# One encoder block on one core: gates moved ahead of the weight splits, GpSimd's tile work taken out of the token tiles and the tail, the router in one fp32 product

## The chip, the core and the metric

The kernel runs on one core of a Trainium2 chip. The metric is the device time of one execution in microseconds; before the change the median of three runs is 2175.32 us (2174.38 to 2176.11). The engines are named as the profile names them: PE is TensorE (PEld is its weight load), DVE is VectorE, ACT is ScalarE, POOL is GpSimd and SP is SyncE, which here only issues DMAs.

## The reference, cut to what matters

The block takes x (1024 tokens x 1024 channels) and computes, in fp32:

- h = RMSNorm(x), z = h @ w_in, whose columns are q, k, v and the two halves a and b of a convolution group.
- Attention over 8 heads with three dilated windows (this part is not touched).
- conv = swish(LayerNorm(depthwise_conv(a * sigmoid(b)))), with a width of 31 over 512 channels.
- x1 = x + concat(attn, conv) @ w_out.
- h2 = RMSNorm(x1) with weight norm2_g; aff = softmax(h2 @ w_router) over 16 experts; each expert takes its 128 highest tokens; y = (silu(h2 @ w1) * (h2 @ w3)) @ w2 for them, times the affinity, added into x1 at the tokens' rows.

## The kernel before

Matrix products of fp32 data are made from two fp32r halves. A tile is split into hi (an ACT copy that rounds) and lo (the difference from the raw tile, on DVE or POOL), and a product is three matmuls: hi*hi, hi*lo, lo*hi (`mm3`, lines 113 to 115). The order of the instructions on PE, ACT and DVE is the program's order (`manual_schedule`); each engine takes its queue in order. POOL's and SP's instructions are placed by the scheduler of the framework, and wait for their tiles.

The stages on which the change bears:

- **Projection and convolution (to about 181 us).** The conv channels are done in four blocks of 128, i = 0 to 3. For each block `z_ab` (line 409) makes b (part 0) and a (part 1), 48 matmuls of 512 columns each. `glu` (line 293) is a generator: b times the norm factor on DVE and a sigmoid on ACT, twice; then the gate times the factor and the product with a on DVE, twice; then a split of the result and 16 DMAs that spread it into the tile U. `conv` (line 329) has nine steps of 12 matmuls. After each step it splits the weights of four steps later (`wc_split`: ACT hi, DVE lo, then a load into the freed ring place from POOL's queue), and after the fifth, ACT copies the first half of the sums out (`left`, line 336). The generator of block i runs one step after each step of conv(i - 1), so that sigmoids and weight splits alternate in ACT's queue. The splits of the next w_ab block (`split_ab`) stand ahead of the loop. The last conv, conv(3), comes after the copy-out and squares of the first q tile.
- **Output projection, token tiles t = 0 to 7 (456.9 to about 593 us).** For each tile of 128 tokens PE makes 48 matmuls of 512 columns (`product`, line 1067), DVE adds the residual (line 1072), and the previous tile gets its norm (`norm`), its transposes (`turned`: 4 PE transposes, an ACT hi copy, an ACT raw copy, a POOL subtraction, line 1092, twice), its router (16 fp32r matmuls whose stationary side is the 32 columns of the split weights, an ACT copy, a PE transpose back, two DVE additions), its softmax, and `kept`: h2 = x1 * r on ACT, times norm2_g on POOL (line 1104), then a DMA to the DRAM tile h2s. In between, DVE sorts the affinities of earlier tiles (`ranked`, with `MAX8`, `MATCH_REPLACE8` and the max/min pairs of lines 986 and 988), in portions that `drip` puts between the other instructions by fixed counts (`DW`, `DL`).
- **The tail (593 to 638.7 us).** The last tile's norm, router and softmax, the last sort, the selection of the 128 tokens of each expert, and the gather of the first expert's rows by an indirect DMA from POOL (line 1412). In this stretch the first two weight tiles of the experts are split with POOL's subtraction (`split_next`), the third on DVE after the indices are known (line 1400).
- **Experts (638.7 us to the end).** For each of 16 experts the gathered rows are transposed (`transposed`: 8 PE transposes, two ACT hi copies and two DVE subtractions of 512 columns), and 33 weight tiles of 128x2048 are loaded, split (lines 1195 and 1196) and multiplied. `load_to` loads them into a ring; a load waits until the tile that had its place is split.

Of the kernel before, what the change touches and what calls it, by code (L numbers as in the profile page):

```python
# [68 lines left out]
def build(ctx, tc, nc, I, out):  # L69
# [77 lines left out]
    wr = sm([P, 8, 2, NE], F32R, "wr")  # L147
# [21 lines left out]
    def router_weights():  # L169
        V.tensor_tensor(wrr, wrr, g2t[:, :, None].to_broadcast([P, 8, NE]), op=ALU.mult)  # L170
        split(wrr, wr[:, :, 0], wr[:, :, 1])
# [121 lines left out]
    def glu(i, pab):  # L293

        sg = sm([P, 2, 512], F32, "sg", tag="tmp4", bufs=1)
# [3 lines left out]
        for half in range(2):  # L299
            c = slice(512 * half, 512 * half + 512)  # L300
            V.tensor_tensor(sg[:, half], pab[0][:, half], rbc[:, c], op=ALU.mult)
            A.activation(sg[:, half], sg[:, half], AF.Sigmoid)
            yield
        ufp = uf.rearrange("p (r t) -> p t r", r=4)
        for half in range(2):
            c = slice(512 * half, 512 * half + 512)
            V.tensor_tensor(sg[:, half], sg[:, half], rbc[:, c], op=ALU.mult)
            V.tensor_tensor(ufp[:, 128 * half:128 * half + 128],
                            pab[1][:, half].rearrange("p (t r) -> p t r", r=4),
                            sg[:, half].rearrange("p (t r) -> p t r", r=4), op=ALU.mult)  # L310
            yield
# [120 lines left out]
    for i in range(4):  # L432
        pab = pab_next
        if i == 0:
            z_ab(0, pab, ((0, 0), (1, 0), (0, 1), (1, 1)))
            pab_next = [psC("pb")]
            A.activation(zeros[:, 0, 1:2], g1[:, 0:1], AF.Sigmoid)
            z_ab(1, pab_next, ((0, 0), (0, 1)), norms_out)
        else:
            if i == 1:  # L440
                pab.append(psS("pa"))
                z_ab(1, pab, ((1, 0), (1, 1)))

                for _ in split_ab(2):
                    pass
                pab_next = [psS("pb")]
                z_ab(2, pab_next, ((0, 0), (0, 1)))
            elif i == 2:
                pab.append(psS("pa"))
                z_ab(2, pab, ((1, 0), (1, 1)))  # L450
            else:
                pab = [psS("pb"), psS("pa")]
                z_ab(i, pab, ((0, 0), (0, 1), (1, 0), (1, 1)))
        while ends:
            ends.pop(0)()
        if i == 2:
            for _ in split_ab(3):
                pass
# [7 lines left out]
        if i == 0:  # L466
            for _ in gates:
                pass
            for n in range(4):
                wc_split(n)  # L470
            continue
        if i == 3:
# [76 lines left out]
    for c in range(2):  # L549
        raw = load_pieces(c + 1)  # L550
        for tp in range(4):
            ps = psS("pqk")
            z_pair(ps, tp, w)
            while ends:
                ends.pop(0)()
# [28 lines left out]
            if (c, tp) == (0, 0):  # L584
                for _ in conv(3, ends):
                    pass
# [377 lines left out]
    misc = slot(4, [D + 2 * P + NT + 2 * NE + 5 * P], F32, "misc")  # L964
    g2 = misc[:, 0:D]
    nc.sync.dma_start(g2, I["g2"].partition_broadcast(P))
    cs = misc[:, D:D + 2 * P + NT + 2 * NE]
# [4 lines left out]
    W, gt, eq = (misc[:, D + 2 * P + NT + 2 * NE + i * P:][:, 0:P] for i in range(3))  # L972
    run = misc[:, D + 5 * P + NT + 2 * NE:].rearrange("p (a k) -> p a k", a=2)
# [55 lines left out]

    xf = misc[:, D + 2 * P + NT + 2 * NE:][:, 0:512]  # L1030
    h2T = slot(11, [2, 8, P], F32R, "h2T")
    ORDER = (0, 1, 4, 5, 2, 6, 7, 3)

    class Token:


        def __init__(self, t):
            self.t, self.xt, self.h2, self.h2T = t, xt2[:, t % 2], h22[:, t % 2], h2T
# [41 lines left out]
        def turned(self, j0, j1, between=None):  # L1080
# [3 lines left out]
            hh, hl = (self.h2T[:, i, j0:j1].rearrange("p j t -> p (j t)") for i in range(2))  # L1084
            A.activation(hh, pt[:, 0:n], AF.Copy)
            if between:
                between()
            if self.last and j0 >= 4:
                V.tensor_tensor(hl, pt[:, 0:n], hh.bitcast(F32), op=ALU.subtract)
            else:  # L1090
                A.activation(xf[:, 0:n], pt[:, 0:n], AF.Copy)
                G.tensor_tensor(hl, xf[:, 0:n], hh.bitcast(F32), op=ALU.subtract)
# [9 lines left out]
        def scaled(self):  # L1102
            A.activation(self.h2[:, 0:D], self.xt, AF.Copy, scale=self.r)
            G.tensor_tensor(self.h2[:, 0:D], self.h2[:, 0:D], g2, op=ALU.mult)

        def router(self, j0=0, j1=8):

            if j0 == 0:
                self.pr = psM("pr")
            for part in range(2):  # L1110
                for j in range(j0, j1):
                    w_ = wr[:, j].rearrange("p a e -> p (a e)")
                    T.matmul(self.pr[0:2 * NE, 0:P], w_, self.h2T[:, part, j], start=j == 0 and not part,
                             stop=j == 7 and part == 1)
            if j1 == 8:
                self.lT = pack[0:2 * NE, (3 + self.t % 2) * P:(4 + self.t % 2) * P]
                A.activation(self.lT, self.pr[0:2 * NE, 0:P], AF.Copy)

        def logits(self):
            pl = psM("pl")  # L1120
            T.transpose(pl[:, 0:2 * NE], self.lT, ident[0:2 * NE, 0:2 * NE])
            self.lg = lg = sm([P, NE], F32, "lg", tag="lg", bufs=2)
            self.sc = sm([P, 4], F32, "rsc", tag="rsc", bufs=2)
            V.tensor_copy(lg, pl[:, 0:NE])
            yield
            V.tensor_tensor(lg, pl[:, NE:2 * NE], lg, op=ALU.add)
            yield
            V.tensor_reduce(self.sc[:, 0:1], lg, axis=AX.X, op=ALU.max)

        def softmax(self, between=lambda: None, prev=None):  # L1130
# [3 lines left out]
            A.activation(af, self.lg, AF.Exp, scale=self.r, bias=sc[:, 1:2], accum_out=sc[:, 2:3])  # L1134
# [178 lines left out]
    prev.kept()  # L1313
# [4 lines left out]
    def split_next(n=1):  # L1318
        for _ in range(n):
            if ahead:  # L1320
                ahead.pop(0)()
# [6 lines left out]
    split_next()  # L1328
    cur.router(6, 8)
    split_next()  # L1330
# [9 lines left out]
    cur.spread()  # L1340
    cur.kept()
    split_next(npre * 2)
# [17 lines left out]
    T.transpose(pt[:, 0:P], half, ident)  # L1360
    drain()
# [24 lines left out]
    for t in range(NT):  # L1386
        T.matmul(rows[:, t * P:(t + 1) * P], to_b[:, t], pos, start=True, stop=True)

# [11 lines left out]
    split_part(npre, 0, 2048, V)  # L1400
# [15 lines left out]
    def transposed(e, xe):  # L1416
        xT = slot(XT[e % 2], [2, 8, P], F32R, "xTe")
        for q in range(2):
            pt = psT("xeT")
            for j in range(4):  # L1420
                T.transpose(pt[:, j * P:(j + 1) * P], xe[:, (4 * q + j) * P:(4 * q + j + 1) * P], ident)  # L1421
            hh = xT[:, 0, 4 * q:4 * q + 4].rearrange("p j t -> p (j t)")
# [104 lines left out]
def layouts(inputs):  # L1527
# [7 lines left out]
    L["g2"] = c(f["norm2_g"].reshape(1, D))  # L1535
# [66 lines left out]
```

## Time and profile before

| what | value |
|---|---|
| median of the timed runs | 2175.32 us |
| the profiled execution, its own time | 2172.52 us |
| its span from first to last instruction | 2170.7 us |
| mean granted PE clock | 0.982 of full |
| busy: PE, DVE, ACT, POOL | 2083.0, 1755.5, 1397.7, 231.0 us |
| chain that ended last | PE 87%, DVE 6%, issue 3%, DMA 2% |

The page gives busy time by engine, a timeline in 40 slices and the chain of work that ended last. Shares over the whole span mix the experts' stage, which is more than two thirds of it, with the stages before it, so the rows below are taken stage by stage. In a timeline row the first number is the start, the second the duration; a group of several instructions is one row with its count, and the bracket at the end says how long the engine was idle before and what released it. A busy matmul is not a matmul at its peak: ends are modelled and overlap the next start, so the pitch from start to start is the cost of one.

### The profile page before, as it was taken

The numbers are of one execution on the slowest core, as the hardware profiler recorded it, in microseconds if no ns is written. First come the engines' busy times: TensorE is split into PE (matmuls) and PEld (weight loads), VectorE is DVE, ScalarE is ACT, GpSimd is POOL, SyncE is SP. The second block draws the span as 40 slices with busy tenths as digits, with TensorE's granted clock in tenths as the row PEclk, the third lists the DMA queues.
The fourth block names the chain that finished last, engine by engine and source line by source line (L and its number), as shares of the span: only waits on it lengthen the run. The fifth ranks groups of instructions, "written<-read, shape, count | busy, mean of one in ns | idle before, by whom it ended". The sixth has DMA issues, their size and how long they took to land.

```text
span 2170.7 us, 27853 instructions
## 1 busy us (share of the span) xinstructions
PE 2083.0 (96%) x10458; PEld 1748.3 (81%) x10458; DVE 1755.5 (81%) x2231; ACT 1397.7 (64%) x1465; POOL 231.0 (11%) x169
## 2 busy tenths in 40 slices
PE   9899999988849999999999999999999999999997
PEld 7888889976638888888888888888888888888886
DVE  6435847868968888888888888888888888888886
ACT  5334735553337777777777777777777777777774
POOL 2110001233230101010010001011010101101010
PEclk9999999999959999999999999999999999999998
DMA  8540158844459999999999999999999999999990
GB/s 290 141 132 25 40 145 168 161 131 178 183 212 346 357 392 371 382 379 374 380 361 387 375 379 384 370 382 363 386 374 376 388 371 382 359 388 378 376 358 10
DMA packets 138743, 647.71 MB, mean 298 GB/s; under 512 B 47984, under 2 KB 52464, under 8 KB 68592
## 3 DMA queue, kind: packets, MB, share of 16 engines
q1 hardware_dynamic: 130688, 617.48, 76.7%
q0 software_dynamic: 7776, 28.45, 4.7%
q8 instruction: 82, 1.34, 0.3%
q14 instruction: 53, 0.43, 0.1%
q10 hardware_dynamic: 144, 0.00, 0.0%
HBM read 607.69 MB, written 21.40 MB: 290 GB/s over the span
## 4 chain that ended last, share of the span: by engine, by line
PE 87%; DVE 6%; issue 3%; DMA 2%; ACT 1%; POOL 0%; SPq 0%; POOLq 0%; ACTq 0%; DVEq 0%
PE w L113 15%; PE w L115 15%; PE w L114 15%; PE y L115 7%; PE y L113 7%; PE y L114 7%; PE pqk L503 4%; PE po L834 2%; PE pv L503 2%; PE hT L1445 2%; PE wo L1067 1%; PE pp L814 1%; PE sc L775 1%; PE sc L776 1%; DVE top L988 1%
## 5 line engine op out<-in xcount | busy, mean ns | idle before, releaser
L1196 DVE TENSOR_TENSOR w<-rw,w 128x2048 fp32r<-128x2048 f32 x527 | 1196.0, 2285 | 183.3 <-ACT w L1195 178.9
L1195 ACT ACTIVATE w<-rw 128x2048 fp32r<-128x2048 f32 (+1 forms) x531 | 1006.9, 1910 | 274.9 <-PE w L115 138.9
L113 PE MATMUL w<-w,xTe 128*128 128x512 f32 (+1 forms) x1536 | 584.4, 380 | 0.0
L115 PE MATMUL w<-w,xTe 128*128 128x512 f32 (+1 forms) x1536 | 574.8, 374 | 0.0
L114 PE MATMUL w<-w,xTe 128*128 128x512 f32 (+1 forms) x1536 | 574.5, 374 | 0.0
L115 PEld LDWEIGHTS w<-w,xTe 128*128 128x128 f32 x1536 | 289.3, 188 | 54.6 <-DVE xTe L1424 0.2
L114 PEld LDWEIGHTS w<-w,xTe 128*128 128x128 f32 x1536 | 289.8, 189 | 51.4
L113 PEld LDWEIGHTS w<-w,xTe 128*128 128x128 f32 x1536 | 289.5, 188 | 51.1 <-ACT xTe L1423 0.4
L115 PE MATMUL y<-w,hts 128*128 128x512 f32 x700 | 276.7, 395 | 0.0
L113 PE MATMUL y<-w,hts 128*128 128x512 f32 x700 | 275.5, 394 | 0.0
L114 PE MATMUL y<-w,hts 128*128 128x512 f32 x700 | 275.2, 393 | 0.0
L114 PEld LDWEIGHTS y<-w,hts 128*128 128x128 f32 x700 | 131.9, 188 | 30.6
L115 PEld LDWEIGHTS y<-w,hts 128*128 128x128 f32 x700 | 131.9, 188 | 29.3
L113 PEld LDWEIGHTS y<-w,hts 128*128 128x128 f32 x700 | 131.9, 188 | 29.1
L1447 ACT ACTIVATE hts<-hT 128x512 fp32r<-128x512 f32 x95 | 53.7, 565 | 112.5 <-PE hT L1445 112.5
L1481 POOL DMA_INDIRECT out_dram<-xy,idx x16 | 78.8, 4927 | 422.9 <-DVE xy L1480 343.5
L1412 POOL DMA_INDIRECT xy<-h2s,idx x16 | 17.6, 1101 | 892.1 <-PE xeT L1421 678.8
L503 PE MATMUL pqk<-wqkv,hT 128*128 128x512 f32 x384 | 89.6, 394 | 0.0
L503 PEld LDWEIGHTS pqk<-wqkv,hT 128*128 128x128 f32 x384 | 72.1, 188 | 16.5
L834 PEld LDWEIGHTS po<-VAB,pT 128*128 128x128 f32 x496 | 59.5, 193 | 5.6 <-DVE pT L818 2.7
L834 PE MATMUL po<-VAB,pT 128*128 128x65 f32 x496 | 59.9, 273 | 4.2 <-DVE pT L818 2.1
L1506 DVE TENSOR_TENSOR sg<-w,sg 128x512 f32<-128x512 f32 x96 | 61.4, 640 | 0.0
(271 smaller groups left out, 2293.0 us busy)
## 6 DMA issues: line engine op xcount, KB each, us to landing
rw<-in_w SPq DMA_DIRECT2D x525, 1024.0 KB
wcraw<-in_wconv POOLq DMA_DIRECT2D x36, 256.0 KB, 4.0
KK<-stg SPq DMA_DIRECT2D x16, 512.0 KB
rawqkv<-in_w_qkv SPq DMA_DIRECT2D x6, 1024.0 KB
h2s<-h SPq DMA_DIRECT2D x8, 520.0 KB
xr<-in_xT SPq DMA_DIRECT2D x8, 512.0 KB
xs<-in_x SPq DMA_DIRECT2D x4, 1024.0 KB
U<-st SPq DMA_DIRECT2D x64, 64.0 KB
```

What stands on the lines that cost most here:

```text
L113: T.matmul(ps, xh, wh, start=start, stop=False)
L114: T.matmul(ps, xh, wl, start=False, stop=False)
L115: T.matmul(ps, xl, wh, start=False, stop=stop_)
L503: T.matmul(ps[:, k], hT[j][:, a % 2, tok], w[j // 2][:, a // 2, j % 2], start=j == 0 and a == 0, stop=j == 7 and a == 2)
L775: T.matmul(ps[:, i, c], q, kh, start=True, stop=False)
L834: T.matmul(po[:, i * VW:(i + 1) * VW], pt[:, i, c], v, start=c == 0, stop=c == 1)
L1195: A.activation(wh, raws[i][:, c0:c1], AF.Copy)
L1196: E.tensor_tensor(wl, raws[i][:, c0:c1], wh.bitcast(F32), op=ALU.subtract)
L1445: T.transpose(pt[:, k * P:(k + 1) * P], h[:, k * P:(k + 1) * P], ident)
L1447: A.activation(hh, pt[:, 0:w], AF.Copy)
L1481: G.indirect_dma_start(out=out[:, :], out_offset=bass.IndirectOffsetOnAxis(ap=idx[:, e:e + 1], axis=0), in_=ys, in_offset=None, compute_op ...
L1506: V.tensor_tensor(sg[:, 0:w], pb[:, 0:w], sg[:, 0:w], op=ALU.mult)
```

## The change

1. `glu` is cut in two. `glu_gate` (b times the factor, sigmoid, times the factor, for both halves) stands right after b is made, ahead of `split_ab`; `glu` keeps the product with a, the split and the spread, one step after each of the first four conv steps. The PE order becomes: a of block i (with the last transposes of conv(i - 2) between its two halves), b of block i + 1, conv(i - 1). Two steps of conv(3) are put ahead of the first q tile's copy-out.
2. The POOL subtraction and the POOL multiplication by norm2_g in the token tiles go. h2s now holds x1 * r without norm2_g; norm2_g is multiplied at the experts' transposes, one 128-column piece at a time. The broadcast load of norm2_g (512 KB) goes.
3. The router is one fp32 product with the tokens as stationary side (8 matmuls of 16 columns into a 128 x 16 tile); the copy, the transpose back and the two additions go, and softmax reads PSUM.
4. The first weight tile's split goes to two halves on DVE, one after the transposes of the last sort, one after the rows' matmuls; the second tile's goes to DVE after the indices, ahead of the third. `kept` of tile 6 moves behind the last tile's `spread`.

```diff
-    for i in range(4):
-        pab = pab_next
...
-        gates = glu(i, pab)
...
+    A.activation(zeros[:, 0, 1:2], g1[:, 0:1], AF.Sigmoid)
+    z_ab(0, pab_next, ((0, 0), (1, 0), (0, 1), (1, 1)))
+    pab, pab_next = pab_next, [psC("pb")]
+    z_ab(1, pab_next, ((0, 0), (0, 1)), norms_out)
+    glu_gate(0, pab[0])
+    for _ in glu(0, pab[1]):
+        pass
+    for n in range(4):
+        wc_split(n)
+    for i in range(1, 4):
+        pab = pab_next
+        glu_gate(i, pab[0])
+        if i == 3:
...
+        else:
+            for _ in split_ab(i + 1):
                 pass
+        pab.append(psS("pa"))
+        z_ab(i, pab, ((1, 0),))
+        end()
+        z_ab(i, pab, ((1, 1),))
+        gates = glu(i, pab[1])
+        if i < 3:
+            pab_next = [psS("pb")]
+            z_ab(i + 1, pab_next, ((0, 0), (0, 1)))
...
         for _ in conv(i - 1, ends):
             next(gates, None)
...
+            if (c, tp) == (0, 0):
+                last_conv = conv(3, ends)
+                for _ in range(2):
+                    next(last_conv)
...
-            hh, hl = (self.h2T[:, i, j0:j1].rearrange("p j t -> p (j t)") for i in range(2))
-            A.activation(hh, pt[:, 0:n], AF.Copy)
+            A.activation(self.h2T[:, j0:j1].rearrange("p j t -> p (j t)"), pt[:, 0:n], AF.Copy)
...
-            if self.last and j0 >= 4:
-                V.tensor_tensor(hl, pt[:, 0:n], hh.bitcast(F32), op=ALU.subtract)
-            else:
-                A.activation(xf[:, 0:n], pt[:, 0:n], AF.Copy)
-                G.tensor_tensor(hl, xf[:, 0:n], hh.bitcast(F32), op=ALU.subtract)
...
             A.activation(self.h2[:, 0:D], self.xt, AF.Copy, scale=self.r)
-            G.tensor_tensor(self.h2[:, 0:D], self.h2[:, 0:D], g2, op=ALU.mult)
...
+                self.pr = psM("pr")[:, 0:NE]
+            for j in range(j0, j1):
+                T.matmul(self.pr, self.h2T[:, j], wrr[:, j], start=j == 0, stop=j == 7)
...
-    npre = 2
-    ahead = [partial(split_part, i, 1024 * hf, 1024 * hf + 1024, G) for i in range(npre) for hf in range(2)]
...
     T.transpose(pt[:, 0:P], half, ident)
+    split_part(0, 0, 1024, V)
...
         T.matmul(rows[:, t * P:(t + 1) * P], to_b[:, t], pos, start=True, stop=True)
+    split_part(0, 1024, 2048, V)
...
-    split_part(npre, 0, 2048, V)
+    split_part(1, 0, 2048, V)
+    split_part(2, 0, 2048, V)
...
-            A.activation(hh, pt, AF.Copy)
-            V.tensor_tensor(xT[:, 1, 4 * q:4 * q + 4].rearrange("p j t -> p (j t)"), pt, hh.bitcast(F32),
-                            op=ALU.subtract)
+            for j in range(4):
+                k, src = 4 * q + j, pt[:, j * P:(j + 1) * P]
+                A.activation(xT[:, 0, k], src, AF.Copy, scale=g2t[:, k:k + 1])
+                V.scalar_tensor_tensor(xT[:, 1, k], src, g2t[:, k:k + 1], xT[:, 0, k].bitcast(F32), op0=ALU.mult,
+                                       op1=ALU.subtract)
```

## Rows read from the trace of the kernel before

**Rows 1.** Windows view: start:end, length, busy (count) by engine, PEclk, DMA share, GB/s.
```profile
488.02:506.31 18.29, 16.42 (x91) 12.77 (x89) 13.74 (x83) 8.71 (x17) 6.85 (x6) 1.00 0.32 120
506.31:525.62 19.31, 14.72 (x79) 11.13 (x78) 18.76 (x97) 7.65 (x15) 5.38 (x5) 1.00 0.68 248
...
560.82:578.49 17.67, 15.48 (x74) 11.82 (x74) 17.11 (x94) 5.05 (x11) 5.34 (x5) 0.90 0.25 91
578.49:595.36 16.87, 13.32 (x96) 11.93 (x96) 16.36 (x87) 6.21 (x13) 5.27 (x5) 0.90 0.91 346
...
735.00:830.00 95.00, 95.00 (x454) 79.04 (x453) 84.11 (x50) 69.81 (x48) 8.33 (x3) 1.00 0.99 382
```

**Rows 2.** Windows view of the four convs, first to last matmul, same columns.
```profile
65.35:80.71 15.36, 13.55 (x113) 13.34 (x112) 10.40 (x16) 7.95 (x16) 3.26 (x6) 1.00 0.33 89
92.22:111.98 19.76, 15.79 (x115) 15.58 (x114) 13.17 (x18) 10.73 (x20) 3.75 (x7) 0.83 0.48 149
134.46:153.64 19.18, 15.14 (x115) 14.93 (x114) 13.41 (x19) 11.57 (x21) 3.75 (x7) 0.91 0.46 148
165.13:181.01 15.88, 13.66 (x116) 13.46 (x114) 10.19 (x23) 6.96 (x13) 0.54 (x1) 1.00 0.06 18
```

**Rows 3.** Timeline of PE in conv(1), the matmul after the fifth step.
```profile
103.56 0.58 PE L357 MATMUL cv<-U,wc 128*128 128x256 f32 x1 [3.97 <-ACT pack L336]
```

**Rows 4.** Timeline of ACT in conv(1), the first of two sigmoids.
```profile
97.73 0.63 ACT L302 ACTIVATE sg<-sg 128x512 f32<-128x512 f32 x1 [2.17 <-DVE sg L301]
```

**Rows 5.** Timeline around the start of block 2's b: its split, its first lo matmul.
```profile
51.49 2.89 DVE L164 TENSOR_TENSOR wabl<-rawab,wabh 128x1024 fp32r<-128x1024 f32 x2
...
54.66 0.39 PE L115 MATMUL pb<-hT,wabl 128*128 128x512 f32 x1
```

**Rows 6.** Timeline of POOL and DVE in token tiles 6 and 7.
```profile
574.12 2.40 POOL L1104 TENSOR_TENSOR h<-h,misc 128x1024 f32<-128x1024 f32 x1
574.16 2.43 DVE L988 TENSOR_TENSOR top<-top 128x64 f32<-128x64 f32 x1
...
577.56 0.22 DVE L988 TENSOR_TENSOR top<-top 128x64 f32<-128x64 f32 x1
...
581.49 1.21 DVE L136 SCALAR_TENSOR_TENSOR rhr<-rha,rhr 128x1 f32<-128x1 f32 x1
```

**Rows 7.** Chain that ended last: start, time, engine, tile, line, count.
```profile
326.75 1.73 PE po L834 x16
...
456.96 15.34 PE wo L1067 x66
...
583.78 0.95 PE pr L1113 x16
```

**Rows 8.** Timeline of PE in the tail: one fp32 matmul of 16 columns, two records.
```profile
627.43 0.61 PE L1396 MATMUL pg<-misc,fm 128*128 128x16 f32 x2 [2.92 <-DVE fm L1393]
```

**Rows 9.** Timeline of DVE in the tail.
```profile
597.85 2.30 DVE L132 TENSOR_TENSOR rha<-rhr 128x1 f32<-128x1 f32 x1
...
610.77 2.77 DVE L1008 TENSOR_TENSOR top<-top 128x64 f32<-128x64 f32 x2
```

**Rows 10.** Timeline of ACT and DVE in the tail, around the last sort's transposes.
```profile
596.58 1.05 ACT L1195 ACTIVATE w<-rw 128x1024 fp32r<-128x1024 f32 x1
...
616.55 0.28 ACT L1357 ACTIVATE top<-sw 128x128 f32<-128x128 f32 x1 [8.06 <-PE sw L1355]
...
617.39 0.29 DVE L1015 TENSOR_TENSOR top<-top,sw 128x128 f32<-128x128 f32 x1 [1.47 <-PE sw L1360]
```

**Rows 11.** Timeline of DVE and POOL at the first gather.
```profile
628.17 2.28 DVE L1196 TENSOR_TENSOR w<-rw,w 128x2048 fp32r<-128x2048 f32 x1
...
628.54 2.83 POOL L1412 DMA_INDIRECT xy<-h2s,idx  x1 [15.08 <-DVE idx L1398]
```

**Rows 12.** All gathers, one line's view: duration ns min/median/max.
```profile
L1412 POOL DMA_INDIRECT xy<-h2s,idx x16: 983/987/2829, 628.5 to 1952.8; - x16
```

**Rows 13.** All scatters, one line's view: duration ns min/median/max.
```profile
L1481 POOL DMA_INDIRECT out_dram<-xy,idx x16: 1549/5594/5616, 749.5 to 2161.0; - x16
```

More of the change, by code (lines that the diff above doesn't have):

```diff
@@ L291, in wc_split, with glu_gate, glu @@
             wc_load(n + 4)
-    def glu(i, pab):
-        sg = sm([P, 2, 512], F32, "sg", tag="tmp4", bufs=1)
+    gate = [None] * 4
+    def glu_gate(i, pb):
+        gate[i] = sg = sm([P, 2, 512], F32, "sg", tag="tmp4", bufs=1)
+        for half in range(2):
+            c = slice(512 * half, 512 * half + 512)
+            V.tensor_tensor(sg[:, half], pb[:, half], rbc[:, c], op=ALU.mult)
+            A.activation(sg[:, half], sg[:, half], AF.Sigmoid)
+        for half in range(2):
+            c = slice(512 * half, 512 * half + 512)
+            V.tensor_tensor(sg[:, half], sg[:, half], rbc[:, c], op=ALU.mult)
+    def glu(i, pa):
         U[i] = slot(20 + i % 2, [2, 4, 264], F32R, "U")
@@ L431, in build, with end @@
     ends = []
-    for i in range(4):
-        pab = pab_next
[L434 to L438, printed above, removed]
-        else:
[L440 to L453, printed above, removed]
+    def end():
         while ends:
             ends.pop(0)()
-        if i == 2:
-            for _ in split_ab(3):
-                pass
+    A.activation(zeros[:, 0, 1:2], g1[:, 0:1], AF.Sigmoid)
[10 more added lines that the diff above has]
+        glu_gate(i, pab[0])
         if i == 3:
@@ L464, in build @@
                 piece_lo(raw, k, w[k])
-        gates = glu(i, pab)
-        if i == 0:
-            for _ in gates:
-                pass
[L469 to L472, printed above, removed]
+        else:
+            for _ in split_ab(i + 1):
+                pass
+        pab.append(psS("pa"))
[6 more added lines that the diff above has]
+            z_ab(i + 1, pab_next, ((0, 0), (0, 1)))
+        else:
             gates = itertools.chain(gates, pieces_late(raw, w))
@@ L553, in build @@
             z_pair(ps, tp, w)
-            while ends:
-                ends.pop(0)()
+            end()
             if tp == 3:
@@ L584, in build @@
             if (c, tp) == (0, 0):
-                for _ in conv(3, ends):
+                for _ in last_conv:
                     pass
@@ L1103, in scaled @@
             A.activation(self.h2[:, 0:D], self.xt, AF.Copy, scale=self.r)
-            G.tensor_tensor(self.h2[:, 0:D], self.h2[:, 0:D], g2, op=ALU.mult)
         def router(self, j0=0, j1=8):
             if j0 == 0:
[L1109 to L1117, printed above, removed]
+                self.pr = psM("pr")[:, 0:NE]
+            for j in range(j0, j1):
+                T.matmul(self.pr, self.h2T[:, j], wrr[:, j], start=j == 0, stop=j == 7)
         def logits(self):
-            pl = psM("pl")
-            T.transpose(pl[:, 0:2 * NE], self.lT, ident[0:2 * NE, 0:2 * NE])
-            self.lg = lg = sm([P, NE], F32, "lg", tag="lg", bufs=2)
             self.sc = sm([P, 4], F32, "rsc", tag="rsc", bufs=2)
-            V.tensor_copy(lg, pl[:, 0:NE])
             yield
-            V.tensor_tensor(lg, pl[:, NE:2 * NE], lg, op=ALU.add)
             yield
-            V.tensor_reduce(self.sc[:, 0:1], lg, axis=AX.X, op=ALU.max)
+            V.tensor_reduce(self.sc[:, 0:1], self.pr, axis=AX.X, op=ALU.max)
         def softmax(self, between=lambda: None, prev=None):
```

42 lines of the change are left out of this document (10 added, 32 removed).

## The prediction

> **What bounds the kernel now.** I read the page's busy table and chain first: PE carries the chain, so only places where PE stands still, or where the work between two PE stretches is serial, can pay. The windows view then sorts the stages. One expert takes 95 us and PE is busy in all of it, while DVE has 11 us and ACT 25 us free [rows 1]; what the change adds there must be hidden to cost nothing, and nothing can be won there. Two stages before it are different.
>
> In the convs, PE's work is the same four times (108 matmuls), yet they last 15.4, 19.8, 19.2 and 15.9 us [rows 2]. In each, PE stops after the fifth step until ACT has copied the first sums out; in conv(1) for 3.97 us [rows 3]. ACT is late there because it takes its queue in order: weight splits, and between them sigmoids, each of which first waits for DVE (2.17 us the first time) [rows 4]. In the two long ones the granted clock is also lower, 0.83 and 0.91 over the stretch, against 1.00 in the short ones [rows 2]: after the longer stop some matmuls run at the lower level.
>
> In the output projection the bound is DVE. From tile 3 on it is busy 17.1 of 17.7 us or 18.8 of 19.3 [rows 1], although PE's matmuls need less. The timeline shows why DVE is so full: a max/min pair member that takes 0.22 us takes 2.43 us when it begins beside a POOL multiplication of 2.40 us, and a one-column operation takes 1.21 us beside a POOL subtraction [rows 6]. So DVE instructions with two SBUF operands are held until POOL's instruction ends.
>
> **The change part by part.** The sum is made against the profiled execution, 2172.52 us (span 2170.7); the timed median lies 2.8 us above it, and I add that at the end.
>
> *Convs.* With the sigmoids gone from the loop, ACT has nine splits, two splits of the gated result and the copy-outs: as little as conv(0) shows or less. What stays is structural: the fifth step's split and the copy-out both wait for PE's fifth step. I take 15.4 us for each, as conv(0) has now [rows 2]: gains of 0, 4.4, 3.8 and 0.5, together 8.7 us (conv(3) because ACT no longer does the q tile's copy and squares ahead of the first two splits). Against it stands the new place of the gates. `glu_gate(1)` puts four DVE instructions and two sigmoids (0.63 us each) [rows 4] ahead of `split_ab(2)`. Its lo halves now run from 51.49 for 2.89 us, two of them, and PE takes the first at 54.66 [rows 5]: the first half is ready some 1.9 us ahead. Four instructions of about 0.6 us and one hop to ACT and back are 3 us, so PE waits about 1.1 us once; between 0.3 and 2.5 with POOL's rope products about. For blocks 2 and 3 the same sits under 11 us of a's matmuls. Sum: -7.6 us; between +1 (the loop is bound by the ring's loads, not by ACT) and -11.
>
> *Token tiles.* Per tile POOL's three instructions go, and with them three DVE holds, about 1.0 + 1.0 + 2.2 = 4.2 us by the rows' excess over 0.15 to 0.22 [rows 6]; two small DVE additions go too (0.2). DVE then needs 17.7 - 4.4 = 13.3 us. PE becomes the longer one: 48 matmuls at 15.34/66 = 0.232 are 11.2 us [rows 7]; the router's 8 fp32 matmuls are two records each, priced at the attention's fp32 products with the same 128x128 stationary side, 1.73/16 = 0.108 a record, so 1.7 us in place of 0.95 [rows 7]; nine transposes at the same 0.1 are 0.9. That is 13.8, and with a short wait for the softmax's transpose 14.2 us. Bounds for the router's record: 0.06, as the old one has (0.95/16), and 0.305, as the lone 16-column fp32 product in the tail has at the lower clock (0.61/2) [rows 8]. I take the nearest form, 0.108. Tiles 4, 5 and 6 (about 17.6 each; the last of them is shown): -3.4 each. Tile 3, with conv pieces on DVE: 19.3 to 15.1, -4.2. Tile 2, where DVE has 4.5 us free and only one hold falls on PE's path [rows 1]: -2. Tile 1 nothing. Sum: -16.5 us (-5 to -20). The scaling of h2 then ends on ACT, which is busy 5 of 17.7.
>
> *Tile 7.* 16.9 us [rows 1], with three holds of the same kind (one is shown) [rows 6], 4.2 us together; DVE then needs 12.7. PE needs 35 matmuls (8.1), one and three quarters routers (3.0) and ten transposes (1.0), about 12, behind the residual. -4.1.
>
> *Last norm to last sort.* Two links of the serial norm each take 2.30 us beside POOL's weight subtractions; one is shown [rows 9]. They become 0.15 each, -4.3, and the copy, the transpose back and the additions behind the router, of which 0.4 is on the path, go: -4.7. In the last sort the pair of line 1008 takes 2.77 in place of 0.36 [rows 9]: -2.4. `kept` of tile 6, moved here, has one ACT scaling (about 1.1 us), two POOL copies of 16 columns and the DMA to h2s; what reads their results, the selection and the gather, comes only after the whole last sort. No cost.
>
> *The splits brought to DVE.* The first half tile stands between the second transpose of the sorted lists and the merge. Its hi (1.05 us) is queued on ACT behind the copy that ends at 616.83, and its lo is half of 2.28, so DVE starts the merge at 616.83 + 1.05 + 1.14 + about 0.1 = 619.1 and not at 617.39 [rows 10, 11]: +1.7 us. The second half falls into DVE's wait for the rows' matmuls, as long as itself within 0.1 us, with its hi long done: nothing. The last two stand back to back behind the indices, 4.5 us, while the gather runs, and DVE has nothing else until its rows land. [...]
>
> *The gather.* It takes 2.83 us where the others take 0.99 [rows 11, 12], and ends 0.92 us after DVE's subtraction does (628.17 + 2.28 = 630.45; 628.54 + 2.83 = 631.37): held for that subtraction. The scatters say the same: 1.55 us at the end of the kernel, 5.59 in the middle, beside two DVE subtractions in a row [rows 13]. With a second subtraction right behind the first I expect it held for both: +2.3 us (0 to 2.3). [...]
>
> *Loads.* Loads 14 and 15 go to the places of weight tiles 0 and 1, so on SP's queue they now wait for the DVE splits (about 15 us later, relative to the stage). Behind them stand only later loads; the indirect DMA and loads 16 and 17 are on POOL's queue. Tile 14 is used eleven tiles after the third, at 95 us for 33 tiles about 32 us into the experts: hidden. The norm2_g load (512 KB) goes; nothing waited for it.
>
> *Experts.* Twelve instructions more per expert on ACT and DVE, under 1 us on each, in 25 and 11 us of free time [rows 1]: nothing. If that cover were gone, 15 times 1 us.
>
> Sum: -7.6 - 16.5 - 4.1 - 4.7 - 2.4 + 1.7 + 2.3 = -31.3, so 2141.2 as a profiled execution, 2144 as a median.
>
> **The rivals.**
>
> *B, the router's fp32 product is dear.* At 0.305 a record it is 4.9 us a tile, PE's floor 17.0 to 17.2. Then tiles 3 to 7 give back about 14 us and tile 2 its 2: 2160. For it: the weight side now changes with every 16 columns. Against it: the same stationary form at full clock costs 0.108 [rows 7].
>
> *C, the convs gain nothing.* If the ring's loads and the splits hold the fifth step, and not the sigmoids, the loop stays at 19 us and the 1.1 us come on top: 2144 + 8.7 = 2153. For it: the load freed by the first step's split lands only shortly before the fifth. Against it: conv(0) has the same ring and lasts 15.4 [rows 2].
>
> *D, the gather is not held twice.* POOL gets in between the two subtractions, as the spread of the scatters' times would allow [rows 13], or a subtraction does not hold it at all: 2144 - 2.3 = 2142. [...]
>
> *E, slower.* The experts' transposes come on PE's path: the next expert's first weight subtractions queue behind eight small pieces on DVE, and the bank that they read is wanted by the next transposes of the hidden rows. It decides from (31.3 + 4.3)/15 = 2.4 us a change of expert; at 3 us it is +45, so 2189. Against it: 11 us of free DVE time in each expert [rows 1].
>
> **How the numbers follow.** The forecast (A) 0.58, with its own range 2136 to 2152; B 0.10; C 0.13; D 0.14; E 0.05. The range 2133 to 2159 takes in C and D and most of B. About 0.2% (4.3 us) is what a measurement of this kernel can tell from no change. Faster: A to D in full but for 0.02, 0.93; same: that 0.02 and the mild end of E, 0.03; slower: the rest of E, 0.04.
>
> **What would show it.** In the new trace: convs of 15 to 16 us with no sigmoid inside; one PE wait of about 1 us ahead of block 2's b; no DVE max/min pair member above 0.5 us in the token tiles; router records at 0.1 us; tile periods near 14 us with PE and not DVE full; the merge of the last sort starting about 1.7 us after its transposes are done; a first gather of about 5 us; experts of 95 us. The prediction is wrong if tile periods stay above 16 us, or if an expert lasts over 96 us.

## The result and the profile after

| | kernel before | changed kernel |
|---|---|---|
| median | 2174.85 us (4 runs) | 2209.78 us (4 runs, 2209.34 to 2215.64) |
| profiled execution, span | 2172.52, 2170.7 us | 2215.64, 2213.8 us |
| first expert's first matmul, in the profile | 638.75 us | 604.73 us |
| from there to the end | 1532.0 us | 1609.1 us |

The ratio is 1.0169, 95% interval 1.0149 to 1.0188: the change made the kernel slower by 35 us, where 31 us less were predicted. The last two rows of the table say where. Up to the experts the changed kernel is 34.0 us ahead, more than the forecast; the experts then take 77.1 us more.

The stages ahead of the experts first. The windows view of the changed kernel, columns as in [rows 1]: the four convs (answering [rows 2]), then one token tile and tile 7 from the transposes of its second half on, then all experts. The row by itself is the kernel before, all experts.

```profile
65.27:80.48 15.21, 13.72 (x114) 13.50 (x113) 8.33 (x12) 7.37 (x14) 3.98 (x8) 1.00 0.50 140
103.00:118.23 15.23, 13.73 (x114) 13.52 (x113) 8.34 (x12) 7.37 (x14) 3.95 (x8) 1.00 0.53 148
129.60:144.81 15.21, 13.72 (x114) 13.51 (x113) 9.81 (x14) 9.14 (x16) 3.91 (x8) 1.00 0.50 138
156.14:171.41 15.27, 13.82 (x116) 13.62 (x115) 10.29 (x23) 6.96 (x13) 0.54 (x1) 1.00 0.07 19
...
541.07:554.95 13.88, 13.88 (x74) 11.66 (x73) 12.79 (x94) 4.00 (x8) 0.38 (x2) 1.00 0.32 115
554.95:567.16 12.21, 12.21 (x97) 11.74 (x95) 9.53 (x68) 2.86 (x7) 0.36 (x2) 1.00 0.75 296
...
604.73:2213.80 1609.07, 1551.55 (x7194) 1273.00 (x7192) 1352.27 (x877) 1128.57 (x847) 94.06 (x46) 0.98 0.91 344
```

```profile
638.75:2170.70 1531.95, 1518.31 (x7193) 1258.68 (x7192) 1331.32 (x781) 1104.39 (x751) 112.84 (x46) 1.00 0.94 360
```

All convs last 15.2 us, at a granted clock of 1.00. In a token tile PE is busy all of its 13.88 us and DVE 12.79: the bound has moved from DVE to PE. In the experts PE stands still for 57.5 us (1609.07 less 1551.55; before, 13.6), and its busy time is 33.2 us longer for the same matmuls. So 43.9 us of the 77.1 are more idle time.

What PE waited for there is in the view of waits, PE's rows within the experts (engine, tile and line, releaser: us in total, times, longest). The kernel before has none of these rows.

```profile
PE y L114 <- DVE w L1175: 20.1, 15, 1.4
PE y L113 <- ACT hts L1420: 15.0, 15, 1.0
PE hT L1418 <- DVE xTe L1397: 7.3, 15, 0.5
```

Each comes 15 times, once per change of expert: 2.8 us a time. The tile `hT` holds transposed hidden rows (the product of an expert's first two weights), and `hts` their split copy. The timelines of ACT and DVE at one such change, from the transposes of the next expert's rows on:

```profile
1184.17 0.37 ACT L1396 ACTIVATE xTe<-xeT,g2t 128x128 fp32r<-128x128 f32 x1 [1.27 <-PE xeT L1393]
1185.52 0.37 ACT L1396 ACTIVATE xTe<-xeT,g2t 128x128 fp32r<-128x128 f32 x1 [0.99 <-DVE xTe L1397]
1186.31 0.37 ACT L1396 ACTIVATE xTe<-xeT,g2t 128x128 fp32r<-128x128 f32 x1 [0.42 <-DVE xTe L1397]
1187.10 0.62 ACT L1396 ACTIVATE xTe<-xeT,g2t 128x128 fp32r<-128x128 f32 x2 [0.42 <-DVE xTe L1397]
...
1189.98 1.91 ACT L1174 ACTIVATE w<-rw 128x2048 fp32r<-128x2048 f32 x1
1191.78 0.59 ACT L1420 ACTIVATE hts<-hT 128x512 fp32r<-128x512 f32 x1
```

```profile
1185.14 0.34 DVE L1397 SCALAR_TENSOR_TENSOR xTe<-xeT,g2t,xTe 128x128 fp32r<-128x128 f32 x1
1185.92 0.35 DVE L1397 SCALAR_TENSOR_TENSOR xTe<-xeT,g2t,xTe 128x128 fp32r<-128x128 f32 x1 [0.43 <-ACT xTe L1396]
...
1191.91 2.29 DVE L1175 TENSOR_TENSOR w<-rw,w 128x2048 fp32r<-128x2048 f32 x1 [1.45 <-ACT w L1174]
```

Read the brackets. A DVE piece waits for the ACT piece whose result it subtracts, as it must. But an ACT piece also waits for the DVE piece before it, though it uses nothing of it: both read the same PSUM tile, and the third experiment below shows that this is what the wait goes by. (The one row of two ACT pieces is where the second PSUM tile begins: its first piece waits for nobody on DVE.) A pair takes 0.79 us (1185.52 to 1186.31), and eight of them hold ACT from 1184.17 to 1190. The weight split that then starts at 1189.98 gives DVE its half at 1191.91, and the copy of the hidden rows stands behind that split on ACT, at 1191.78. PE waits first for that copy and then for DVE's half:

```profile
1187.90 0.66 PE L1418 MATMUL hT<-ident,sg 128*128 128x128 f32 x4 [0.47 <-DVE xTe L1397]
...
1192.42 0.50 PE L113 MATMUL y<-w,hts 128*128 128x512 f32 x1 [1.01 <-ACT hts L1420]
1194.26 0.51 PE L114 MATMUL y<-w,hts 128*128 128x512 f32 x1 [1.34 <-DVE w L1175]
1194.86 0.50 PE L115 MATMUL y<-w,hts 128*128 128x512 f32 x1
```

At a change of expert of the kernel before, ACT is through with the rows after 1.0 us, and its weight split follows:

```profile
1193.56 1.09 ACT L1423 ACTIVATE xTe<-xeT 128x512 fp32r<-128x512 f32 x2 [1.27 <-PE xeT L1421]
1194.53 1.91 ACT L1195 ACTIVATE w<-rw 128x2048 fp32r<-128x2048 f32 x1
```

```profile
1194.53 1.28 DVE L1424 TENSOR_TENSOR xTe<-xeT,xTe 128x512 fp32r<-128x512 f32 x2
```

Part of the rest of the loss is the clock. At the next change, 100 us later, the windows view shows PE idle and then, with PE busy again (5.81 of the 6 us from 1293), a granted clock of 0.50:

```profile
1291.00:1293.00 2.00, 0.50 (x1) 0.19 (x1) 2.00 (x1) 2.00 (x3) 1.25 (x1) 0.88 0.03 10
1293.00:1295.00 2.00, 1.81 (x4) 1.30 (x5) 2.00 (x3) 2.00 (x2) 0.18 (x1) 0.50 0.55 98
1295.00:1297.00 2.00, 2.00 (x7) 1.52 (x6) 2.00 (x3) 0.17 (x1) 0.00 (x0) 0.50 0.90 377
1297.00:1299.00 2.00, 2.00 (x6) 1.60 (x5) 1.47 (x1) 0.54 (x1) 0.00 (x0) 0.50 0.94 365
```

Windows of 10 us show such a fall at 8 of the 15 changes; at 1192 there is none. Of the 33.2 us of longer busy time some 19 are the lower clock (busy time by what is missing from 1.00, summed over those windows). The other 14 are not: from one expert's transposes to the next's, the changes without a fall take 98.6 or 98.9 us where the kernel before takes 94.5 or 95.0, so each loses 4.0 us at the full clock, 2.9 of them idle. The records above show where busy time grows: the matmuls at the two stops last 0.50 or 0.51 us, where those right behind them last 0.39 or 0.40, and one starts 0.6 us after the one ahead of it, in place of 0.23 (1194.26 to 1194.86).

### The profile page after: what moved, and what is told of

The parts are those of the page before. It is cut to its first block, busy times and chain, and to the rows that moved or that the text cites. A ratio compares the mean times of both kernels' runs of the same rounds, so it can differ in the third digit from the quotient of the medians.

```text
span 2213.8 us, 27951 instructions
## 1 busy us (share of the span) xinstructions
PE 2110.4 (95%) x10450; PEld 1765.0 (80%) x10450; DVE 1747.1 (79%) x2311; ACT 1413.8 (64%) x1536; POOL 163.5 (7%) x142
## 4 chain that ended last, share of the span: by engine, by line
PE 81%; DVE 7%; ACT 3%; issue 2%; DMA 1%; POOLq 0%; ACTq 0%; DVEq 0%
PE w L115 14%; PE w L113 14%; PE w L114 14%; PE y L115 7%; PE y L114 7%; PE y L113 7%; PE pqk L501 4%; PE wo L1064 4%; DVE w L1175 3%; PE po L835 2%; PE pv L501 2%; PE hT L1418 2%; ACT w L1174 2%; PE pp L815 1%; DVE xTe L1397 1%
## 5 line engine op out<-in xcount | busy, mean ns | idle before, releaser
L1175 DVE TENSOR_TENSOR w<-rw,w 128x2048 fp32r<-128x2048 f32 (+1 forms) x530 | 1200.2, 2281 | 199.5 <-ACT w L1174 195.1
L114 PE MATMUL y<-w,hts 128*128 128x512 f32 x700 | 284.7, 407 | 20.1 <-DVE w L1175 20.1
L113 PE MATMUL y<-w,hts 128*128 128x512 f32 x700 | 282.9, 404 | 15.0 <-ACT hts L1420 15.0
L115 PE MATMUL y<-w,hts 128*128 128x512 f32 x700 | 286.1, 409 | 0.9
L114 PEld LDWEIGHTS y<-w,hts 128*128 128x128 f32 x700 | 136.0, 194 | 56.3 <-DVE w L1175 24.8
L113 PEld LDWEIGHTS y<-w,hts 128*128 128x128 f32 x700 | 136.5, 195 | 48.4 <-ACT hts L1420 18.1
L115 PEld LDWEIGHTS y<-w,hts 128*128 128x128 f32 x700 | 136.3, 195 | 35.7 <-DVE hts L1421 5.8
L1454 POOL DMA_INDIRECT out_dram<-xy,idx x16 | 67.8, 4240 | 516.4 <-DVE xy L1453 434.7
L1396 ACT ACTIVATE xTe<-xeT,g2t 128x128 fp32r<-128x128 f32 x128 | 45.3, 367 | 84.8 <-DVE xTe L1397 48.8
L1397 DVE SCALAR_TENSOR_TENSOR xTe<-xeT,g2t,xTe 128x128 fp32r<-128x128 f32 x128 | 43.4, 349 | 47.5 <-ACT xTe L1396 47.5
L163 DVE TENSOR_TENSOR wc<-wcraw,wc 128x512 fp32r<-128x512 f32 x36 | 26.0, 733 | 63.5 <-ACT wc L162 63.5
```

Source lines behind the costliest of these rows:

```text
L113: T.matmul(ps, xh, wh, start=start, stop=False)
L114: T.matmul(ps, xh, wl, start=False, stop=False)
L115: T.matmul(ps, xl, wh, start=False, stop=stop_)
L1175: E.tensor_tensor(wl, raws[i][:, c0:c1], wh.bitcast(F32), op=ALU.subtract)
L1396: A.activation(xT[:, 0, k], src, AF.Copy, scale=g2t[:, k:k + 1])
L1397: V.scalar_tensor_tensor(xT[:, 1, k], src, g2t[:, k:k + 1], xT[:, 0, k].bitcast(F32), op0=ALU.mult, op1=ALU.subtract)
```

## The experiments

Theory 1: the exchange between ACT and DVE over one PSUM tile, piece by piece, starves the weight splits. Its rivals: the added instructions are too much work (theory 2); loads 14 and 15 come late (theory 3); the transposes hold their bank too long (theory 4).

**Pieces grouped by engine.** The same sixteen instructions, another order:

```diff
             for j in range(4):
                 k, src = 4 * q + j, pt[:, j * P:(j + 1) * P]
                 A.activation(xT[:, 0, k], src, AF.Copy, scale=g2t[:, k:k + 1])
+            for j in range(4):
+                k, src = 4 * q + j, pt[:, j * P:(j + 1) * P]
                 V.scalar_tensor_tensor(xT[:, 1, k], src, g2t[:, k:k + 1], xT[:, 0, k].bitcast(F32), op0=ALU.mult,
                                        op1=ALU.subtract)
```

> The changed kernel, with the pieces of the experts' transposes in another order: for each half, the four ACT pieces first and the four DVE pieces behind them, in place of ACT, DVE, ACT, DVE. The instructions are the same, in number and shape. Theory 1 (each ACT piece waits for the DVE piece before it, because both read one PSUM tile; the exchange of eight pairs at 0.79 us delays the weight splits): three of four waits go, an expert comes back from 100 us to 95 or 96, and the kernel to 2138 to 2155 us, below the kernel before. Theory 2 (the sixteen small instructions themselves are too much work for ACT and DVE): 2200 to 2212 us, as the changed kernel. Theory 3 (loads 14 and 15, and all behind them, come late) and theory 4 (the bank that the transposes fill is wanted by the hidden rows' transposes) : also near 2210, as the loads are untouched and the bank is held about as long.

Measured: 2142.54 us, ratio to before 0.9859 (0.9843 to 0.9875). Theory 1 holds; 2 and 3 fall, since instructions and loads are the changed kernel's. Theory 4 does not fall by this run: grouped, DVE is through with the tiles 3.3 us after ACT's first piece (1158.66 to 1161.99) and alternating after 6.3 (1184.17 to 1190.46), so the PSUM tiles come free sooner too. What theory 4 can be worth is in the view of waits: the row of 7.3 us, of 42.4. ACT and DVE at a change of expert, and the windows view of all experts:

```profile
1158.66 2.17 ACT L1396 ACTIVATE xTe<-xeT,g2t 128x128 fp32r<-128x128 f32 x8 [1.27 <-PE xeT L1393]
1160.67 1.97 ACT L1174 ACTIVATE w<-rw 128x2048 fp32r<-128x2048 f32 x1
...
1159.83 2.16 DVE L1399 SCALAR_TENSOR_TENSOR xTe<-xeT,g2t,xTe 128x128 fp32r<-128x128 f32 x8
```

```profile
602.87:2138.00 1535.13, 1521.24 (x7194) 1256.67 (x7192) 1343.84 (x877) 1120.28 (x847) 110.39 (x46) 1.00 0.94 361
```

Eight ACT pieces take 2.17 us in place of 5.8, and the weight split follows 2.0 us after the first piece. PE is idle for 13.9 us of the 1535.1, as before the change.

**The norm weights alone, on the kernel before.** One edit of the change by itself:

```diff
-            G.tensor_tensor(self.h2[:, 0:D], self.h2[:, 0:D], g2, op=ALU.mult)
...
-            A.activation(hh, pt, AF.Copy)
-            V.tensor_tensor(..., pt, hh.bitcast(F32), op=ALU.subtract)
+            for j in range(4):  # as in the changed kernel
```

> The kernel before, with only the norm weights moved: the POOL multiplication of the normalised rows is taken out, and the experts' transposes multiply by them, in the changed kernel's alternating pieces. Theories 1 and 2: the whole loss of the changed kernel's experts stands here, 71 to 77 us, less what the missing POOL multiplication gives the token tiles (one DVE hold of about 2.2 us in each of tiles 3 to 6): 2230 to 2242 us. Theory 3 (late loads): the loads are as in the kernel before, so the experts stay at 95 us and the time falls by about 5 to 9 us, to 2166 to 2172. Theory 4: as theories 1 and 2.

Measured: 2238.19 us, ratio 1.0290 (1.0269 to 1.0311). The whole loss stands in this one edit, with the loads of the kernel before, so theory 3 falls again. Its first expert starts at 625.68, 13.1 us sooner than before (the POOL multiplication is gone; 5 to 9 were expected), and its experts take 83.2 us longer than before, 6 more than in the changed kernel, and those 6 are longer busy time of PE (1558.1 us, in the changed kernel 1551.6) and no more idle time (57.0 us, there 57.5). PE's waits are those of the changed kernel:

```profile
PE y L114 <- DVE w L1195: 20.1, 15, 1.4
PE y L113 <- ACT hts L1447: 15.1, 15, 1.0
PE hT L1445 <- DVE xTe L1424: 7.3, 15, 0.5
```

**Pieces alternating, the two PSUM tiles in turn.** This asks what the wait goes by: the PSUM tile that both read, or the SBUF tile that both write, or alternation as such.

```diff
+        pts = [psT("xeT") for _ in range(2)]
...
+        for j in range(4):
+            for q in range(2):
+                k, src = 4 * q + j, pts[q][:, j * P:(j + 1) * P]
```

> The changed kernel, with the pieces still alternating one by one between ACT and DVE, but taken in turn from the two PSUM tiles: an ACT piece then has in front of it a DVE piece of the other tile, and the DVE piece of its own tile lies one pair further back. Theory 1 (the wait goes by PSUM tile): the pairs overlap, the pitch falls from 0.79 us towards the 0.37 of an ACT piece, and most of the loss goes: 2145 to 2180 us. If instead the wait comes from the shared SBUF tile of the results, or from the alternation as such, or the work is too much (theory 2): 2200 to 2212, as the changed kernel.

Measured: 2162.55 us, ratio 0.9947 (0.9929 to 0.9965). ACT at a change of expert:

```profile
1168.34 0.80 ACT L1397 ACTIVATE xTe<-xeT,g2t 128x128 fp32r<-128x128 f32 x2 [1.27 <-PE xeT L1393]
1169.70 0.62 ACT L1397 ACTIVATE xTe<-xeT,g2t 128x128 fp32r<-128x128 f32 x2 [0.55 <-DVE xTe L1398]
1170.48 0.62 ACT L1397 ACTIVATE xTe<-xeT,g2t 128x128 fp32r<-128x128 f32 x2 [0.16 <-issue]
1171.27 0.63 ACT L1397 ACTIVATE xTe<-xeT,g2t 128x128 fp32r<-128x128 f32 x2 [0.16 <-DVE xTe L1398]
```

ACT now does two pieces, one of each tile, in each 0.79 us: 3.5 us in place of 5.8. The SBUF tile is the same for all eight, so the wait goes by the PSUM tile. The experts take 1555.2 us, at a clock of 1.00: 23.3 of the 77.1 are left.

```profile
605.40:2160.60 1555.20, 1528.88 (x7194) 1257.26 (x7192) 1347.31 (x877) 1125.51 (x847) 108.09 (x46) 1.00 0.94 356
```

The row of theory 4 (`hT` behind `xTe`) is still there in full, 7.3 us in 15 places, while DVE's half of the weights now costs PE 3.7 us and the copy of the hidden rows nothing. So theory 4 is part of the loss, and the smaller one: PE is idle for 12.7 us more than before and busy for 10.6 more, here without any fall of the clock at the changes of expert.

**The gates alone, on the kernel before**: `glu_gate`, the new order and the two conv steps ahead, nothing else.

> The kernel before, with only the first part of the change: the gates apart from the splits, the new order of the matmuls, and the last conv two steps ahead. By the two traces (the next block's products begin at 181.01 us before and at 171.25 in the changed kernel) it is worth 9.8 us: 2164 to 2167 us. The prediction's step was 7.6 us: 2167. If the convs' gain came from another part of the change, such as the router, it stays at 2174 to 2175.

Measured: 2166.47 us, ratio 0.9965 (0.9953 to 0.9978), 7.9 us less (4.8 to 10.2 by the interval). In its profile the products after conv(3) begin at 171.65 us, 9.4 sooner than before, so the convs' part does not come from the rest of the change.

**Whole halves**: the changed kernel with one copy and one subtraction of 512 columns per half; it leaves the norm weights out of the experts.

```diff
-            for j in range(4):
-                ...  # pieces with scale=g2t
+            A.activation(hh, pt, AF.Copy)
+            V.tensor_tensor(..., pt, hh.bitcast(F32), op=ALU.subtract)
```

> The changed kernel with the experts' transposes as they were before: one ACT copy and one DVE subtraction of 512 columns for each half. It leaves the norm weights out of the experts. Theory 1 (only the exchange piece by piece costs, not the added instructions): as the kernel with the pieces grouped by engine, within 4 us of its 2142.5; its experts lasted 1535.1 us in place of 1531.9, so at most 3 us are left for sixteen small instructions in place of four. Theory 2 (the added instructions themselves have a price even when grouped): 8 us or more below 2142.5.

Measured: 2140.68 us, ratio 0.9845 (0.9830 to 0.9860), 1.9 us below the grouped pieces (3.8 below their second measurement, 2144.50). Its experts take 1531.6 us, the grouped ones 1535.1: sixteen small instructions in place of four cost 0.2 us an expert. That is what theory 2 is worth.

**The tail's two steps.** Three variants of the grouped kernel size two terms of the sum. In the first, ACT's half of the first half tile goes ahead of the last sort and DVE's right behind it; in the second, the two DVE subtractions beside the gather go behind the first expert's transposes; the third has both.

```diff
+    split_part(0, 0, 1024, V, lo=False)
     for _ in falling(NT - 1, last):
         drip()
+    split_part(0, 0, 1024, V, hi=False)
...
-    split_part(1, 0, 2048, V)
-    split_part(2, 0, 2048, V)
+    split_part(1, 0, 2048, V, lo=False)
+    split_part(2, 0, 2048, V, lo=False)
...
     xT = transposed(0, xe)
+    split_part(1, 0, 2048, V, hi=False)
+    split_part(2, 0, 2048, V, hi=False)
```

> The kernel with the pieces grouped, and the first half tile of the weights split earlier: its ACT half ahead of the last sort, its DVE half right behind the sort, into DVE's wait for the two transposes and the copy between them. The prediction's step put 1.7 us on the merge for this half; the changed kernel's trace shows 1.55. If the step is right, the merge starts 1.3 us after the transposes' start (as before the change) and the time falls by 1.5 us, to 2141. If DVE's half delays what the transposes need, the gain is gone: 2142.5 or above.

> The kernel with the pieces grouped, and the two DVE subtractions that run beside the first gather put behind the first expert's transposes (ACT's halves stay). If a DVE subtraction holds the gather, the gather falls from 2.28 to 1.0 us and the first expert's first matmul comes 1.3 us sooner: 2141 us. If 2.28 is the first gather's own time, whatever DVE does, it stays at 2.28, and the time is as without the edit or later, since the second and third weight tiles are split later: 2142 to 2146.

> Both of these edits on the kernel with the pieces grouped. If both steps are as said, 2.8 us below 2142.5, that is 2139 to 2140. If the gather or the half tile gains nothing, 2141 to 2143.

Measured: 2144.41, 2142.28 and 2141.07 us (ratios 0.9863, 0.9846 and 0.9840, each within 0.0016). By their times all three missed: the first was to fall to 2141, the second too, and the third to 2139 to 2140. These times do not tell the edits apart, but the traces do. In the grouped kernel and then in the one with the gather undisturbed, the indices, the gather and the first expert's first matmul:

```profile
592.70 0.17 DVE L1369 CAST idx<-pg 128x16 int32<-128x16 f32 x1 [0.70 <-PE pg L1367]
592.79 4.48 DVE L1175 TENSOR_TENSOR w<-rw,w 128x2048 fp32r<-128x2048 f32 x2
593.71 2.28 POOL L1384 DMA_INDIRECT xy<-h2s,idx  x1 [23.17 <-DMA rw<-in_w]
602.87 0.79 PE L113 MATMUL w<-w,xTe 128*128 128x512 f32 x1
```

```profile
598.79 0.17 DVE L1371 CAST idx<-pg 128x16 int32<-128x16 f32 x1 [0.70 <-PE pg L1369]
599.80 1.04 POOL L1386 DMA_INDIRECT xy<-h2s,idx  x1 [23.16 <-DMA rw<-in_w]
605.54 0.51 PE L113 MATMUL w<-w,xTe 128*128 128x512 f32 x1
```

From the indices to the first matmul it is 10.17 us and then 6.75: 3.4 us less, 1.24 of them the gather itself. With the half tile moved, the merge of the last sort comes 1.33 us after the first transpose's start (578.78 to 580.11) in place of 2.87 (579.23 to 582.10), and the first expert's matmul 1.4 us sooner after that start (22.20 in place of 23.64). With both, the stretch from that transpose to the first expert's matmul is 18.68 us in place of 23.64. Yet the profiled span with both edits is not shorter but 1.9 us longer (2139.9, and 2138.0 grouped). One reason lies in the earlier stages, which the edits do not touch, and which vary: the output projection began at 447.6 us in the grouped kernel's profile and at 451.2 in the one with both. So the two were timed again side by side:

> The kernel with the pieces grouped by engine, timed again on one chip together with the next kernel, since five microseconds between them are to be told apart: 2142.5 us, as before.

> The same with the early half tile and the undisturbed gather. By the traces the stretch from the last sort's transposes to the first expert's first matmul is 5.0 us shorter (18.68 in place of 23.64), but the profiled run began that stretch 5.2 us later, in stages that the edits do not touch, at a lower granted clock. If that was the run and not the edits, the median is 4 to 5 us below the grouped kernel's, near 2138. If the edits themselves make the earlier stages later, the profile again shows the output projection beginning near 451 us in place of 447.6, and the medians lie within 2 us.

Measured: 2144.50 and 2140.99 us, ratios 0.9865 (0.9850 to 0.9881) and 0.9839 (0.9825 to 0.9853). This time the output projection began at 450.3 us in the grouped kernel and at 447.3 in the one with both: the start varies with the run. The stretch itself is again shorter, 18.79 us in place of 24.01. The medians differ by 3.5 us, less than expected (4 to 5, and near 2138). Each of the five runs with both edits was faster than each of the four without, but the intervals overlap, so by the times the gain is likely and not shown. The traces also show why not all of 5 us can arrive: from the first expert's first matmul to the second expert's transposes it is 80.4 us in both grouped profiles and 81.9 in both with the edits. In the kernel with the gather undisturbed, 81.9 too, PE waits in that stretch 1.2 us for a late subtraction of the weights and 0.5 for DVE's pieces. So the second edit gives back about 1.5 us of what it brings. With both edits the kernel has the lowest median of those that keep all of the computation: 1.6% below before, by both measurements.

## Why the prediction was wrong

By its own steps, first expert's matmul by first expert's matmul, in the profiled executions:

| step | predicted | measured | by |
|---|---|---|---|
| convs | -7.6 | -9.8 | next product after conv(3): 181.01, then 171.25 |
| on to the output projection | | +0.6 | its start: 456.96, then 447.75 |
| token tiles | -16.5 | -15.1 | second transposes of tile 7: 579.23, then 554.95 |
| tile 7 | -4.1 | -3.9 | its last residual piece: 595.36, then 567.16 |
| last norm | -4.7 | -4.5 | softmax's product: 604.30, then 571.64 |
| last sort | -2.4 | -2.4 | first transpose: 616.06, then 580.99 |
| first half split | +1.7 | +1.6 | merge: 617.39, then 583.87 |
| second half, gather | +2.3 | -0.5 | first expert's matmul: 638.75, then 604.73 |
| **experts** | **0** | **+77.1** | end of the span: 2170.7, then 2213.8 |

By its own sign (an expert over 96 us) the prediction was wrong: the changed kernel's take 98.6 to 101.6 us.

*The step that failed* is "Twelve instructions more per expert on ACT and DVE, under 1 us on each, in 25 and 11 us of free time: nothing." The work was sized about right: grouped, the pieces take 2.17 us on ACT and 2.16 on DVE, where the two copies and two subtractions of the kernel before take 1.1 and 1.3, and they cost 0.2 us an expert. The wait was not counted: alternating, the pieces held ACT for 5.8 us, and the experts took 77.1 us longer in place of nothing. Busy time was set against free time, and nobody asked what each piece waits for, nor what stands behind it on its engine. The place was in the diff: ACT and DVE alternate over one PSUM tile. The whole halves of the kernel before alternate too, but only twice, and there the DVE subtraction needs the copy anyway.

The wait goes by the tile: pieces of two tiles in turn lose 23 us, of one tile 77. No run here tells tile and bank apart or shows what makes the wait, and what would happen without it was not tried. The trace of the kernel before does not show it: with whole halves, ACT is idle ahead of its copies for 38.5 us in 16 places, and each time until PE's transposes are done, never until DVE is.

*Rival E* had the place (PE waits at the change of expert, behind the pieces), and its second half is the row of 7.3 us, hidden rows' transposes waiting for DVE's pieces. But it was priced at 3 us a change and given 0.05, because 11 us of DVE time are free in an expert. That is the same fault: free time on average is no argument about a queue at one moment. The 77.1 us over 15 changes are 5.1 us each, of which 2.9 idle.

*The convs* won more than forecast. The wait ahead of block 2's b, +1.1 us, did not come: the gates' four DVE instructions took 3.5 us, more than the 3 forecast, but DVE came to them at 49.71, 1.8 us sooner than it came to this split before (51.49 in [rows 5]). The split's first half was ready at 54.4 with b's first need at 54.6, so of the 1.9 us of lead 0.2 were left. That DVE would be early was not in the forecast: here the wait stayed out by luck. And all stops after the fifth step are 1.5 us; in conv(1), against [rows 3]:

```profile
111.79 0.38 PE L360 MATMUL cv<-U,wc 128*128 128x256 f32 x1 [1.50 <-ACT pack L339]
```

*The token tiles and the router*: 13.9 us a tile against 14.2 forecast for tiles 4 to 6 (from one tile's second transposes to the next's). What is short of the forecast is tile 1, which was put at nothing and takes 14.6 us in place of 13.5. The bound is PE, with the router at 1.69/16 = 0.106 us a record (0.108 taken) and rival B out. From the chain of the changed kernel, against [rows 7]:

```profile
447.75 15.36 PE wo L1064 x66
...
543.96 1.69 PE pr L1101 x16
```

*The tail*: the link of [rows 9] at 2.30 us is 0.16, and the pair of 2.77 is 0.36. The half split costs what was said:

```profile
568.79 0.16 DVE L132 TENSOR_TENSOR rha<-rhr 128x1 f32<-128x1 f32 x1
...
578.11 0.36 DVE L1007 TENSOR_TENSOR top<-top 128x64 f32<-128x64 f32 x2
...
582.72 1.23 DVE L1175 TENSOR_TENSOR w<-rw,w 128x1024 fp32r<-128x1024 f32 x1 [1.88 <-ACT w L1174]
583.87 0.28 DVE L1014 TENSOR_TENSOR top<-top,sw 128x128 f32<-128x128 f32 x1
```

*The gather* was expected to be held for both subtractions, and it was held for one. In the changed kernel, against [rows 11]:

```profile
594.56 4.48 DVE L1175 TENSOR_TENSOR w<-rw,w 128x2048 fp32r<-128x2048 f32 x2
...
595.48 2.27 POOL L1384 DMA_INDIRECT xy<-h2s,idx  x1 [23.17 <-DMA rw<-in_w]
597.76 1.13 POOL L158 DMA_DIRECT2D rw<-in_w  x2
```

It ends at 597.75, 0.9 us after the first of the two subtractions does (594.56 + 2.28 = 596.84), as in [rows 11], and before the second one's end (599.04). So it gets in between them: rival D's first form. The scatters of [rows 13], from which the forecast argued, show both: beside two subtractions in a row three of them took 3.39 us before the change and twelve about 5.6. Rival D's other form, that a subtraction does not hold it at all, falls for this gather: with DVE idle it takes 1.04 us. It does not fall for every DMA that POOL issues. The two plain weight loads right behind the gather lie wholly beside the second subtraction, and take 1.13 us together, as they do with DVE idle (1.14). Why the one is held and the other not was not tried.

With the experts' step right the forecast would have held: the grouped kernel, 2142.5 and 2144.5 us, is the kernel that the prediction describes (2144). That it comes so close is partly luck: in its first profile it is 35.9 us ahead at the first expert's first matmul, 4.6 more than the forecast of 31.3, and loses 3.2 in the experts, where nothing was forecast.

## What to carry to other kernels

Before free busy time is taken as cover for small instructions, write down for each what it waits for and what queues behind it: a chain over two engines costs its hops and not only its work (here 0.79 us a pair, for pieces of 0.37 and 0.35). Pieces that two engines read out of one PSUM tile should be issued engine by engine, which cost 0.2 us an expert here, and not alternating over one tile (5.1 us); two tiles in turn lie between (1.5 us). And here, where PE had run without a gap, a wait cost more than itself: 2.9 us of idle time a change came to 5.1, in part because matmuls behind it ran at a granted clock of 0.50.

## What the runs showed of the hardware that was not expected

- An exchange between ACT and DVE costs 0.79 us a pair for pieces of 128x128, where the same pieces, eight in a row on one engine, take 2.17 us, 0.27 each.
- 43.9 us of waits, in 15 places, came with 33.2 us of longer matmul time, some 19 of them at the lower clock and 14 at the full one; the granted clock was 0.50 from 1293 to 1299 with PE busy for 5.81 of the 6 us, and 8 of 15 changes of expert show such a fall.
- An undisturbed gather brought 3.4 us, not the 1.3 of the gather itself. From its end to the first transpose it took 5.2 us (595.99 to 601.17) and then 3.5 (600.84 to 604.30), and the first expert's first matmul took 0.79 us and then 0.51, the clock being 0.50 and 1.00 at that point. The clock is not what makes the difference: in the second measurement of both edits that matmul took 0.79 us again, and the gap was 3.6 us (5.6 grouped). In the slower case SP's weight loads moved 3.15 MB in the 16 us around it; without the early subtractions 1.05 MB in 12 us. That these loads delay the gathered rows is an argument, not a test.
- A subtraction on DVE held POOL's indirect gather (2.27 us beside it, 1.04 without) and not POOL's plain loads (1.13 us for two beside it, 1.14 without).
- The stages ahead of the output projection vary by some 5 us from run to run (its start lay between 447.1 and 452.2 us in kernels that share these stages). In the three that began after 450 us the granted clock between 440 and 450 us was 0.66 or 0.67, in the four others for which it was read 0.83 to 1.00; edits of a few microseconds need the trace of their own stretch, not the span.
